# Moving the first 8 MB load ahead of the program's opening barrier in a ReLU-and-row-sum kernel

## The chip, the cores and the metric

The kernel runs on one core of one Trainium2 chip. The metric is the device time of one execution in microseconds (us).

"Span" is the time from the first to the last of the program's own instructions in the profile. A semaphore is a counter that an engine raises, or waits for: in the trace of the kernel before SyncE's drain at 0.00 us raises one, and its barrier instruction at 0.65 us waits for another. A packet is one piece of a DMA transfer as the profiler recorded it.

## The reference

```python
x = randn(32, 512, 1024)            # float32, 67.11 MB
out = sum(maximum(x, 0), axis=-1)   # (32, 512) float32
```

The 16,384 rows are laid out as 128 partitions of 128 rows each. One row has 1,024 numbers, 4 KB.

## The kernel before

The kernel streams the input through two buffers of 16 rows per partition (8 MB each). SyncE issues every load. ScalarE takes the even rows and VectorE the odd ones; each instruction applies the ReLU and sums a row. The last rows come in smaller loads, so that little work is left after the last one lands.

```python
    big = 16
    tail = [8, 4, 2, 1]
    pieces = [244, 252, 260, 268]
    ...
    io_pool = ctx.enter_context(tc.tile_pool(name="io", bufs=2))
    ...
    for j, cpd in enumerate(chunks):
        ...
        nc.sync.dma_start(
            out=xt,
            in_=xv[:, m0 * D : (m0 + cpd) * D].rearrange("p (c d) -> p c d", c=cpd),
        )
        for c in range(cpd):
            ...
            elif (c % 2) == 0:
                act_op(xt[:, c, :], xt[:, c, :], m)
            else:
                dve_op(xt[:, c, :], xt[:, c, :], res[:, m : m + 1])
```

The program has an opening that the kernel's author doesn't write. GpSimd sets four small constants. Then all five engines meet in a barrier: the other four each run an instruction called drain, which adds one to a semaphore, and wait; GpSimd sees that the four have come (at 0.53 us in the trace of the kernel before) and releases them (at 0.61). Only then do the engines branch to the kernel's body, whose first SyncE instruction is the first load.

## Time and profile before

| | before |
|---|---|
| device time, median of the first 3 runs | 164.37 us |
| span in the profile | 162.7 us |
| SyncE's first load issued | 0.73 us after the span's start |
| first DMA packet starts | 1.74 us |
| all of the first load landed | 23.18 us |

The page of the kernel before, cut to four lines: the span; each engine's busy time with its share of the span and its instructions; SyncE's DMA queue with packets, MB and the share of 16 engines' span; and what was moved:

```profile
span 162.7 us, 347 instructions
...
DVE 74.3 (46%) x134; ACT 69.0 (42%) x129; POOL 0.2 (0%) x4
...
q1 hardware_dynamic: 2304, 67.11, 96.4%
...
HBM read 67.11 MB, written 0.07 MB: 413 GB/s over the span
```

The compute engines (DVE is VectorE, ACT is ScalarE) are idle more than half of the time. SyncE's DMA queue is busy for 96.4% of all that 16 DMA engines could do. This kernel is a stream, and the stream is what must end earlier.

The timeline of the kernel before, first 3 us. Columns: start, duration, engine, line, operation, operands, count, and in brackets the engine's idle time with what ended it:

```profile
0.24 0.10 POOL L113 MEMSET const-float32-0.0<- 128x1 f32 x1 [0.24 <-issue]
...
0.72 1.28 ACT L41 ACT_TABLE_LOAD   x1 [0.72 <-PEq L113]
0.73 0.85 SPq L65 DMA_DIRECT2D xt<-in_x_dram  x2
```

Nothing moves before 0.73 us: the constants are set from 0.24 us on, and ScalarE and SyncE both start just after the barrier. "SPq" is SyncE's sequencer; the line merges the issues of the first two loads.

The view of waits of SyncE's queue, kernel before. Columns: total, how often, longest:

```profile
SPq L65 <- DVE xt L49: 126.5, 6, 30.8
...
SPq L113 <- PEq L113: 0.7, 1, 0.7
```

The 126.5 us are waits for a free buffer. They look large and cost nothing: the third load is issued at 32.5 us, ten us before the second one has landed (42.7 us), so the DMA engines never run dry (their busy share from 40 to 150 us is 0.99). The 0.7 us wait in the barrier is small, and it is the one that matters, because nothing at all is queued while it lasts.

### The profile page before, as it was taken

The page shows a single profiled execution, that of the slowest core. Times are in us where ns is not written, and L with a number is a line of the kernel's source. Part 1 is how long each engine was busy: PE and PEld are TensorE (multiplying, and loading weights), DVE is VectorE, ACT ScalarE, POOL GpSimd, SP SyncE. Part 2 cuts the span into 40 slices and gives each one's busy share as a digit, 9 for nine tenths or more (in the row PEclk, how much of TensorE's full clock was granted, in tenths as well). Part 3 has the DMA queues.
Part 4 walks back from the last instruction along what each step waited for, and adds up shares of the span by engine and source line. Part 5 has one row for each costly group of instructions (what it writes and reads, how often), then busy time and mean ns, then how long its engine had stood idle before and what let it go on. Part 6 is the DMA issues. An engine that isn't in the chain of part 4 may idle for free.

```text
span 162.7 us, 347 instructions
## 1 busy us (share of the span) xinstructions
DVE 74.3 (46%) x134; ACT 69.0 (42%) x129; POOL 0.2 (0%) x4
## 2 busy tenths in 40 slices
DVE  0000029900597007950099300992039900598983
ACT  3000029700595007930099100990039700596882
POOL 0000000000000000000000000000000000000000
DMA  7969969969969979979989998998997997999990
GB/s 258 483 290 516 499 274 516 499 274 516 500 274 516 516 306 467 516 338 435 516 356 421 499 403 387 516 419 354 516 467 306 516 467 306 451 443 395 405 362 23
DMA packets 2450, 67.19 MB, mean 413 GB/s; under 512 B 528, under 2 KB 1040, under 8 KB 1168
## 3 DMA queue, kind: packets, MB, share of 16 engines
q1 hardware_dynamic: 2304, 67.11, 96.4%
q10 hardware_dynamic: 144, 0.06, 0.1%
q14 instruction: 2, 0.02, 0.0%
HBM read 67.11 MB, written 0.07 MB: 413 GB/s over the span
## 4 chain that ended last, share of the span: by engine, by line
DMA 78%; DVE 18%; SPq 1%; issue 0%; DVEq 0%
DMA xt<-in_x_dram 62%; DVE xt L49 17%; DMA p<-in_x_dram 17%; SPq L65 1%; DVE p L49 1%; DVEq L49 0%; DVEq L124 0%
## 5 line engine op out<-in xcount | busy, mean ns | idle before, releaser
L49 DVE TENSOR_SCALAR_CACHE_REDUCE xt<-xt 128x1024 f32<-128x1024 f32 x63 | 72.6, 1215 | 85.7 <-DMA xt<-in_x_dram 85.4
L41 ACT ACTIVATE xt<-xt 128x1024 f32<-128x1024 f32 x64 | 66.7, 1043 | 90.3 <-DMA xt<-in_x_dram 90.3
L41 ACT ACTIVATION_READ_ACCUMULATOR xt<-xt 128x1 f32 x64 | 11.9, 186 | 0.0
L49 DVE DVE_READ_ACCUMULATOR xt<-xt 128x1 f32 x63 | 5.2, 83 | 0.0
L49 DVE TENSOR_SCALAR_CACHE_REDUCE p<-p 128x244 f32<-128x244 f32 (+3 forms) x4 | 1.6, 420 | 0.5 <-DMA p<-in_x_dram 0.4
L41 ACT ACT_TABLE_LOAD x1 | 1.3, 1283 | 0.7 <-PEq L113 0.7
L49 DVE DVE_READ_ACCUMULATOR p<-p 128x1 f32 x4 | 0.3, 83 | 0.0
L113 POOL MEMSET const-bfloat16-1.0<- 128x1 bf16 x1 | 0.1, 102 | 0.0
L113 POOL MEMSET const-uint8-127<- 128x1 uint8 x1 | 0.1, 101 | 0.0
L113 POOL MEMSET const-float32-0.0<- 128x1 f32 x1 | 0.1, 99 | 0.2 <-issue 0.2
L113 POOL MEMSET const-float32-1.0<- 128x1 f32 x1 | 0.1, 98 | 0.0
## 6 DMA issues: line engine op xcount, KB each, us to landing
xt<-in_x_dram SPq DMA_DIRECT2D x1, 4096.0 KB, 19.7
xt<-in_x_dram SPq DMA_DIRECT2D x1, 2048.0 KB, 24.2
xt<-in_x_dram SPq DMA_DIRECT2D x1, 1024.0 KB, 26.2
xt<-in_x_dram SPq DMA_DIRECT2D x1, 512.0 KB, 27.0
p<-in_x_dram SPq DMA_DIRECT2D x1, 134.0 KB, 10.0
p<-in_x_dram SPq DMA_DIRECT2D x1, 130.0 KB, 26.5
p<-in_x_dram SPq DMA_DIRECT2D x1, 126.0 KB, 26.7
p<-in_x_dram SPq DMA_DIRECT2D x1, 122.0 KB, 26.9
```

The lines of the kernel that those rows point to most:

```text
L41: nc.scalar.activation(out=out_ap, in_=in_ap, func=mybir.ActivationFunctionType.Relu, accum_out=res[:, m : m + 1],)
L49: nc.vector.tensor_scalar(out=out_ap, in0=in_ap, scalar1=0.0, scalar2=None, op0=mybir.AluOpType.max, op1=mybir.AluOpType.add, accum_out=ac ...
L65: nc.sync.dma_start(out=xt, in_=xv[:, m0 * D : (m0 + cpd) * D].rearrange("p (c d) -> p c d", c=cpd),)
L113: nc = _bacc.Bacc("TRN2", target_bir_lowering=False, num_devices=1)
```

## The change

The intent is to hide the opening barrier. By the program, the first load needs nothing that the barrier protects: its buffer is untouched, its source is an input, and its semaphore is at zero. (That is reasoning.) So its issue is taken out of the body once the program has been compiled, and put ahead of SyncE's drain in the opening.

```diff
+EARLY = 1
+
+def tile_relu_sum_kernel(tc, x, out):
+    trace_relu_sum(tc, x, out)          # the old kernel function, renamed
+    tc.close()
+    tc.compile()
+    issue_ahead_of_the_barrier(tc, EARLY)
+
+def issue_ahead_of_the_barrier(tc, n_loads):
+    SP = mybir.EngineType.SP
+    blocks = tc.nc.main_func.blocks
+    opening = blocks[0].instructions
+    body = next(b for b in blocks if b.name == tc.start_bb_name).instructions
+    loads = [i for i in body if i.engine == SP][:n_loads]
+    for i in loads:
+        assert isinstance(i, mybir.InstDMACopy)
+        body.remove(i)
+    at = next(n for n, i in enumerate(opening)
+              if i.engine == SP and isinstance(i, mybir.InstDrain))
+    opening[at:at] = loads
```

(Blank lines, type annotations and line breaks are left out here. In this diff and those below, what stands behind a # was added for this document.) No instruction is added or taken away: both profiles count 347.

More of the change, by code (lines that the diff above doesn't have):

```diff
@@ L6, with kernel, issue_ahead_of_the_barrier, trace_relu_sum @@
 from concourse._compat import with_exitstack
+EARLY = 1
+def kernel(tc: tile.TileContext, x: bass.AP, out: bass.AP):
+    trace_relu_sum(tc, x, out)
+    tc.close()
+    tc.compile()
+    issue_ahead_of_the_barrier(tc, EARLY)
+def issue_ahead_of_the_barrier(tc: tile.TileContext, n_loads: int):
+    SP = mybir.EngineType.SP
[6 more added lines that the diff above has]
+        body.remove(i)
+    at = next(
+        n
+        for n, i in enumerate(opening)
+        if i.engine == SP and isinstance(i, mybir.InstDrain)
+    )
+    opening[at:at] = loads
 @with_exitstack
-def kernel(
+def trace_relu_sum(
     ctx: ExitStack,
```

## The prediction

Two passages are cut from it, as marked. 164.37 us, less 0.73 us for the moved issue, plus up to 0.05 us for a colder first issue, is about 163.7 us.

> **What bounds the kernel now.** It is a stream: the page shows 67.11 MB read, the DMA queue of SyncE busy for 96.4% of 16 engines' span of 162.7 us, VectorE 46% and ScalarE 42%. In the steady part the packet records show 64 KB packets of 2.42 us on each of 16 engines, which is 433 GB/s[...]. At 433 GB/s the 67.11 MB take 155 us, so about 7.7 us of the span are start, ramp and tail. The view of waits shows compute waiting for loads (85.4 us VectorE, 90.3 us ScalarE). SyncE's queue waits 126.5 us for buffers, but the third load is issued 10 us before the second has landed (32.5 against 42.7 us), the later ones likewise, so the engines always have a load queued.
>
> **The start.** In the trace SyncE is the first engine in the program: its part of the opening barrier is at 0.00 us, VectorE's, ScalarE's and GpSimd's first instructions at 0.13, PE's at 0.32. GpSimd then sets four constants (0.24 to 0.43), drains until 0.48, gathers at 0.53 and releases at 0.61; SyncE passes at 0.65. It issues the first load at 0.73 (0.38 us, timeline) and the first packet starts at 1.74, 1.01 us after the issue began.[...]
>
> **The change** adds and removes no instruction; it moves the first load's issue from 0.73 us to SyncE's first slot, about 0.00. Removed from the critical path: 0.73 us. Cost: SyncE now arrives at the barrier after its 0.38 us issue, near 0.40 instead of 0.00. PE arrives at 0.32 and GpSimd looks only at 0.53, so the release should stay at 0.61. The second load stays at about 0.73 us, long before it is needed.
>
> The load's start heads a stream without gaps, so all of it should shift rigidly: first landing (before: 23.2 us) to about 22.45, the third load's issue from 32.5 to about 31.75, and the end likewise. Ramp and tail stay. Gain 0.73 us, less perhaps 0.05 for a colder first issue (estimate: the first issue takes 0.38 us, the third 0.33).
>
> **Prediction: 163.7 us** (164.37 less about 0.7, 0.4%), range 163.3 to 164.3. Chances: faster by over 2% 0.01, within 2% 0.98, slower by over 2% 0.01.
>
> **What would show it.** Right: first load issued within 0.1 us of the span's start, first packet near 1.0 us, barrier release still near 0.6 us, the landings and the last instruction 0.6 to 0.75 us earlier, span near 162.0, steady rate unchanged. Wrong: release of the barrier later by the issue's 0.38 us (costs nothing unless it is much more); first packet further than 1.1 us behind its issue; the shift present at the first landing and gone by the last one.
>
> **What would make it wrong.** (a) SyncE's drain in the barrier waits until the 8 MB have landed: then all engines start near 22 us, the second load is issued only then, and the DMA engines idle for one issue-to-packet latency, about 1 us net. (b) In the timed executions another engine enters first, or the metric's clock starts so as to hide the gain. (c) An engine-level straggler or a fetch of instructions near the end absorbs it. (d) Drift between runs: 0.3% is 0.5 us, nearly the effect.

## The result, and the profile after

Ratios below are the mean time of one kernel's fast runs over that of the other's of the same rounds, so they are not quite the ratio of the medians that stand beside them.

| | before | after |
|---|---|---|
| device time, median (lowest to highest), 4 runs each | 164.34 (164.23 to 164.52) | 163.32 (163.30 to 163.39) |
| ratio | | 0.9941 (0.9927 to 0.9955) |
| span in the profile | 162.7 | 161.5 |
| first load issued | 0.73 | 0.00 |
| first DMA packet starts | 1.74 | 1.02 |
| first load landed | 23.18 | 22.24 |

The page of the changed kernel:

```profile
span 161.5 us, 347 instructions
...
DVE 74.3 (46%) x134; ACT 69.0 (43%) x129; POOL 0.2 (0%) x4
...
q1 hardware_dynamic: 2304, 67.11, 96.9%
...
HBM read 67.11 MB, written 0.07 MB: 416 GB/s over the span
```

The same work and the same bytes in a span that is 0.7% shorter. The interval of the ratio excludes 1, and this gain is what is explained here. The timeline of the changed kernel, first 3 us:

```profile
0.00 1.11 SPq L95 DMA_DIRECT2D xt<-in_x_dram  x2
0.23 0.10 POOL L143 MEMSET const-float32-0.0<- 128x1 f32 x1 [0.23 <-issue]
...
0.78 1.28 ACT L71 ACT_TABLE_LOAD   x1 [0.78 <-PEq L143]
```

The first issue is now the first thing that happens. The barrier opens slightly later: ScalarE's table load begins at 0.78 us where it began at 0.72. In the trace's records SyncE's drain behind the issue takes 0.13 us, so SyncE reaches the barrier at 0.56 us and has become the last to arrive. And SyncE's queue hardly waits in the barrier any more (view of waits, SyncE's queue, changed kernel):

```profile
SPq L95 <- DVE xt L79: 125.8, 6, 30.4
...
SPq L143 <- PEq L143: 0.2, 1, 0.2
```

So the mechanism looks as forecast. The size doesn't quite: 1.02 us were gained in the medians and 1.17 us between the two profiles, and the issue moved by only 0.73 us. The timelines of both kernels at the first landing, before and then after, show that more than 0.73 us has gone by then:

```profile
23.20 1.22 DVE L49 TENSOR_SCALAR_CACHE_REDUCE xt<-xt 128x1024 f32<-128x1024 f32 x1 [23.20 <-DMA xt<-in_x_dram]
```

```profile
22.27 1.22 DVE L79 TENSOR_SCALAR_CACHE_REDUCE xt<-xt 128x1024 f32<-128x1024 f32 x1 [22.27 <-DMA xt<-in_x_dram]
```

That is 0.93 us. The rest is in the stream itself. Here is the view by windows, 40 to 150 us, of before, then of after (columns: window, its length, busy time and count of VectorE, ScalarE, GpSimd, granted clock, DMA share, GB/s):

```profile
40.00:150.00 110.00, 55.37 (x97) 50.72 (x97) 0.00 (x0) 1.00 0.99 427
```

```profile
40.00:150.00 110.00, 56.55 (x99) 51.90 (x99) 0.00 (x0) 1.00 1.00 432
```

The stream of this one profile of the kernel before ran at 427 GB/s and that of the changed kernel at 432. Nothing in the change touches this stretch. Either these extra 0.3 to 0.4 us are scatter, or the opening has an effect on the stream that I had not seen. That is the question for the experiments.

### The profile page after: what moved, and what is told of

Same layout as the page of the kernel before. It is cut to its first block, busy times and chain, and to the rows that moved or that the text cites. A ratio compares the mean times of both kernels' runs of the same rounds, so it can differ in the third digit from the quotient of the medians.

```text
span 161.5 us, 347 instructions
## 1 busy us (share of the span) xinstructions
DVE 74.3 (46%) x134; ACT 69.0 (43%) x129; POOL 0.2 (0%) x4
## 4 chain that ended last, share of the span: by engine, by line
DMA 79%; DVE 18%; SPq 1%; issue 0%; DVEq 0%
DMA xt<-in_x_dram 62%; DVE xt L79 17%; DMA p<-in_x_dram 17%; SPq L95 1%; DVE p L79 1%; DVEq L79 0%; DVEq L16 0%
## 5 line engine op out<-in xcount | busy, mean ns | idle before, releaser
L79 DVE TENSOR_SCALAR_CACHE_REDUCE xt<-xt 128x1024 f32<-128x1024 f32 x63 | 72.6, 1216 | 84.5 <-DMA xt<-in_x_dram 84.2
```

Of the source, the lines that this page charges most:

```text
L79: nc.vector.tensor_scalar(out=out_ap, in0=in_ap, scalar1=0.0, scalar2=None, op0=mybir.AluOpType.max, op1=mybir.AluOpType.add, accum_out=ac ...
```

## The experiments

**Theory A.** The whole stream shifts rigidly with the first issue; only the time of that issue counts. What is beyond 0.73 us is scatter, of the profile of before and of its runs.

**Theory B.** The order of the opening also changes how fast the first loads run. In the kernel before the second issue follows the first at once (0.43 us from start to start); in the changed one it stands 0.78 us behind it. A second issue close behind might slow the first load.

**Theory C.** Being ahead of the barrier helps by itself, whatever the time of the issue, through what runs beside the first packets.

An overview; times in us. "Issue" and "barrier" (when ScalarE passes it) are from each run's trace, "landed" is the landing of the first 8 MB less the time of the first issue.

| run | issue | barrier | landed | median (lowest to highest) | ratio to before |
|---|---|---|---|---|---|
| e1: before, unchanged | 0.73 | 0.65 | 22.31 | 163.90 (163.76 to 164.17) | 0.9986 |
| e4: before, gap between the issues | 0.73 | 0.65 | 22.43 | 164.18 (163.89 to 164.32) | 0.9995 |
| e6: early, held back | 0.58 | 1.28 | 22.52 | 163.98 (163.78 to 164.26) | 0.9993 |
| e5: load late | 3.01 | 0.65 | 22.53 | 166.38 (166.35 to 166.84) | 1.0145 |
| e2: after, unchanged | 0.00 | 0.69 | 22.40 | 163.32 (163.26 to 163.80) | 0.9954 |
| e10: after, unchanged | 0.00 | 0.71 | 22.27 | 163.20 (163.15 to 163.28) | 0.9948 |
| e3: two early | 0.00 | 1.17 | 22.24 | 163.38 (163.14 to 163.49) | 0.9950 |
| e7: barrier late | 0.00 | 2.98 | 22.23 | 163.50 (163.40 to 163.63) | 0.9963 |
| e9: small first load | 0.00 | 1.17 | 21.62 | 163.36 (162.98 to 163.67) | 0.9958 |
| e8: two queues | 0.00 | 1.41 | 42.76 | 183.49 (183.20 to 183.63) | 1.1178 |

All gave correct results. The kernel before, run beside them, had medians of 164.19 (e1 to e4), 164.13 (e5 to e8) and 164.13 (e9, e10).

### e1 and e2: both kernels again

No edit. Expected of e1:

> The kernel before, unchanged, run as if it were a change, to see how much its runs, spans and first landing scatter. The move of the issue explains 0.73 us; 1.02 us was measured, and the two profiles differ by 1.17 us in span: 0.73 in the issue, 0.21 more by the first landing, 0.15 more by the second. Theory A (only the shift of the issue counts; the rest is scatter of the one profile and of the runs of before): this run's profile differs from the first one by 0.2 us or more in span, and issue to first landing is anywhere between 22.2 and 22.5 us. Theory B (the opening's order also changes how fast the first loads run): issue to first landing is again 22.4 to 22.5 us, span again 162.6 to 162.8, ratio 1.000.

Expected of e2:

> The changed kernel again, on the same chip as the others. Both theories: about 163.3 us, span 161.5. Theory B: issue to first landing again 22.2 to 22.3 us; theory A: it may be anything from 22.2 to 22.5.

Measured: e1 has a span of 162.1 us in its profile, 0.6 us less than the first profile of the very same program. The ratio of e1 to the same kernel beside it is 0.9986 (0.9972 to 1.0000), so even the means of a batch differ by 0.2 us. First issue to first landing is 22.31 us, not the 22.45 of the first profile; it lies between the changed kernel's 22.24 and 22.40. The same window of e1:

```profile
40.00:150.00 110.00, 55.98 (x97) 51.34 (x97) 0.00 (x0) 1.00 0.99 429
```

and of e2, the changed kernel again:

```profile
40.00:150.00 110.00, 56.05 (x97) 51.39 (x97) 0.00 (x0) 1.00 1.00 430
```

The streaming rate is 427 and 429 GB/s in two profiles of before, 432 and 430 in two of after: the ranges nearly meet, and in e2 the profiled run was the slowest span of its five (162.0; the others 161.5 to 161.7). The first profile of before, 162.7, was slower than all 34 later runs of that kernel (162.0 to 162.6). Of e2's expectation, the 163.3 us came true; its profiled run had a span of 162.0 where 161.5 was expected, and 22.40 us to the first landing where theory B asked for 22.2 to 22.3. This speaks for theory A: most of the extra gain of the first comparison was one unlucky profile and a high batch. Why that batch of the kernel before lay high is not known.

### e3: two loads ahead of the barrier

```diff
-EARLY = 1
+EARLY = 2
```

> Both of the first two loads are issued ahead of the barrier, back to back as in the kernel before (about 0.43 us apart; 0.78 in the changed kernel). Theory A (pure shift): 163.3 us, as the changed kernel, since the second load is not needed for 20 us. Theory B (a second issue close behind the first slows the start of the first load): issue to first landing back to 22.4 to 22.5 us, about 163.6 us.

Measured: 163.38 us, and 22.24 us to the first landing, with the two issues 0.42 us apart. Timeline of e3:

```profile
0.00 0.84 SPq L95 DMA_DIRECT2D xt<-in_x_dram  x2
...
1.24 1.28 ACT L71 ACT_TABLE_LOAD   x1 [1.24 <-PEq L143]
```

The issues are as close together as before the change, and the gain is still there. Theory B's prediction (163.6 us) is missed. The barrier now opens about half a us later than in the changed kernel and that isn't seen in the time either.

### e4: a gap between the issues, behind the barrier

The first load is put behind SyncE's part of the barrier, and a pause of seven empty drains follows it:

```diff
+    for _ in range(7):                 # made before the tile context
+        nc.sync.drain()
...
-    at = next(
+    at = 1 + next(
...
-        if i.engine == SP and isinstance(i, mybir.InstDrain)
+        if i.engine == SP and isinstance(i, mybir.InstEventSemaphore)
```

> The first load stays behind the barrier, and seven empty drain instructions on SyncE stand between it and the second one, so that the two issues are about 0.8 us apart as in the changed kernel. Theory A: 164.3 us, as before. Theory B: about 164.05 us, issue to first landing 22.2 to 22.3 us.

Measured: 164.18 us (before beside it: 164.19), 22.43 us to the first landing, issues 0.91 us apart. Timeline of e4, the two issues and VectorE's first work:

```profile
0.73 1.24 SPq L95 DMA_DIRECT2D xt<-in_x_dram  x2
...
23.18 1.22 DVE L79 TENSOR_SCALAR_CACHE_REDUCE xt<-xt 128x1024 f32<-128x1024 f32 x1 [23.18 <-DMA xt<-in_x_dram]
```

A gap alone brings nothing. Theory B falls with e3 and e4 together: the spacing was taken from either kernel into the other, and the time stayed with the time of the first issue.

### e5: the load much later

```diff
+    for _ in range(44):                # behind the barrier, ahead of the first load
+        nc.sync.drain()
     with _tile.TileContext(nc) as tc:
```

> The kernel before with 44 empty drain instructions on SyncE between the barrier and the first load's issue; seven of them took 0.48 us in the last batch, so the issue should be about 3.0 us later, at 3.75 us. Theory A (the stream shifts rigidly with the first issue): 3.0 us slower than before, 167.2 us, spans and landings all 3.0 us later. Rival (some of the issue's time is hidden, or is paid more than once): a slope clearly off 1, under 2.6 or over 3.4 us.

Measured: 166.38 against 164.13 us, 2.25 us slower. The expectation of 3.0 us was wrong, and 2.25 us even lies below the 2.6 us that it set as the mark of a rival; but both were worked out for a move of 3.0 us, and the issue moved less. A drain took 0.052 us here, not the 0.069 that I had worked out from e4 (where the first one stands behind an issue; in the changed kernel such a drain takes 0.13 us). The timeline of e5 shows where the issue and the first landing came to be:

```profile
3.01 0.84 SPq L65 DMA_DIRECT2D xt<-in_x_dram  x2
...
25.56 1.22 DVE L49 TENSOR_SCALAR_CACHE_REDUCE xt<-xt 128x1024 f32<-128x1024 f32 x1 [25.56 <-DMA xt<-in_x_dram]
```

The issue moved by 2.28 us (3.01 less 0.73), the time by 2.25 us in the medians and 2.4 us by the ratio (1.45% of 164.13). The slope that theory A asks for is 1, and it is 1 within the scatter.

### e6: ahead of the barrier, but not earlier

Eleven drains ahead of the early load:

```diff
-    opening[at:at] = loads
+    opening[at:at] = pauses + loads    # pauses: 11 drains, moved here from behind the barrier
```

> The changed kernel, but eleven empty drains stand ahead of the early load, so it stays ahead of SyncE's part of the barrier and is issued at about 0.75 us, as in the kernel before; the barrier then opens at about 1.3 us. Theory A (only the time of the issue counts): 164.2 us, as before, issue-to-first-landing 22.2 to 22.5. Rival C (being ahead of the barrier helps by itself, by what runs beside the first packets, such as the table load of ScalarE): about 163.9 us or less.

Measured: 163.98 us against 164.13 for before beside it, ratio 0.9993 (0.9980 to 1.0006). The drains held it less than meant: the issue stands at 0.58 us, so 0.15 us of the move were left, and theory A with that time gives 163.98. Timeline of e6:

```profile
0.58 1.10 SPq L99 DMA_DIRECT2D xt<-in_x_dram  x2
1.35 1.28 ACT L75 ACT_TABLE_LOAD   x1 [1.35 <-PEq L147]
```

The load is ahead of the barrier in program order, the table load comes well behind the issue, and the gain is gone but for what the 0.15 us explain. Theory C expected about 163.9 us or less for a full hold of 0.75 us. As the hold was shorter, A and C come within 0.1 us of each other here, and this run doesn't separate them as sharply as meant; it leaves C no effect larger than the scatter.

### e7: the barrier much later, the load not

```diff
-    opening[at:at] = loads
+    opening[at:at] = loads + pauses    # pauses: 44 drains
```

> The changed kernel with 44 empty drains between the early load and SyncE's part of the barrier: the load is issued at 0.00 as in the changed kernel, and all engines and the second load are held until about 3.6 us instead of 0.7. Theory A: 163.3 us, as the changed kernel, since no engine is needed before the first landing at 22.2 us and no second load before about 20 us. Rival (the barrier's time is on the path): up to 3 us slower.

Timeline of e7:

```profile
0.00 3.38 SPq L99 DMA_DIRECT2D xt<-in_x_dram  x2
...
3.05 1.28 ACT L75 ACT_TABLE_LOAD   x1 [3.05 <-PEq L147]
...
22.26 1.22 DVE L83 TENSOR_SCALAR_CACHE_REDUCE xt<-xt 128x1024 f32<-128x1024 f32 x1 [22.26 <-DMA xt<-in_x_dram]
```

Measured: 163.50 us. The barrier opened 2.3 us later than in the changed kernel and the second load was issued at 3.06 us; VectorE's first work begins at 22.26 us, as in the changed kernel (22.27). The 0.18 us above the changed kernel's 163.32 are no more than two batches of one kernel differ by (e1). With e5 this is the clearest pair: 2.3 us of delay in front of the load cost 2.25 us, 2.3 us of delay behind it cost 0.18 us, which the scatter can account for.

### e8: two queues (a try for a faster version, failed)

In the traces the 16 DMA engines take their first packets over 0.9 to 1.3 us. I tried to shorten this ramp with a second issuer.

```diff
+        if j == 0:
+            nc.sync.dma_start(out=xt[0:64], in_=src[0:64])
+            nc.scalar.dma_start(out=xt[64:128], in_=src[64:128])   # both ahead of the barrier
```

From the expectation a condition is cut that named a cause of the ramp.

> A try for a faster version: the first load is split by partitions, 0 to 63 issued by SyncE and 64 to 127 by ScalarE, both ahead of the barrier. In the traces so far the 16 DMA engines take their first packet over 0.9 to 1.3 us after the first of them. [...]two queues shorten it and the first landing comes up to 0.4 us earlier: about 163.0 us. If it doesn't, 163.3 us.

Measured: 183.49 us, 19 us slower. The page of e8, GB/s in 40 slices of the span, and the two queues:

```profile
GB/s 231 231 231 231 231 231 216 188 173 346 462 462 462 433 418 375 390 462 462 462 462 433 418 364 404 462 462 462 447 447 404 404 375 462 418 433 393 417 391 40
...
q1 hardware_dynamic: 2240, 62.92, 86.3%
q10 hardware_dynamic: 224, 4.26, 11.0%
```

The first load moved at half rate until about 40 us, 231 GB/s in most slices where later ones have up to 462: its 64 KB packets took 4.92 us where others take 2.42. The packet records of e8 show that its two halves were moved in turns: 16 packets of SyncE's queue start at 1.34 to 2.00 us, then 16 of ScalarE's at 5.89 to 7.21 us, then 16 of SyncE's at 10.82 to 12.14 us, and so on in eight such turns. Why a packet takes twice as long in them was not shown: e8 has both a cut by partitions and a second queue, and no run has one without the other. The expectation had thought of neither the turns nor the longer packets: it was about how soon the first packets start.

### e9 and e10: a small first load, and the changed kernel once more

The same ramp, cut by rows instead of partitions, on the one queue:

```diff
-EARLY = 1
+EARLY = 2
...
+        if j == 0:
+            nc.sync.dma_start(out=xt[:, 0:2, :], in_=src[:, 0:2, :])
+            nc.sync.dma_start(out=xt[:, 2:cpd, :], in_=src[:, 2:cpd, :])
```

> A second try for a faster version: the first load is cut by rows, 2 rows of each partition (8 KB pieces, 1 MB) and then 14 rows, both issued by SyncE ahead of the barrier on the one queue. In the changed kernel the first 64 KB packets take 3.0 us in the mean, the later ones 2.42, and the 16 engines start theirs over 0.9 to 1.3 us. If the ramp grows with the size of the first pieces, all engines are running full earlier and the first landing of all 16 rows comes up to 0.4 us before 22.2 us: about 163.0 us. If it is a fixed latency of the first pieces, 163.3 us.

> The changed kernel a third time, on the same chip as the cut load. From the eight kernels so far (two queues left out) the time is 163.4 us plus 1.02 us for each us by which the first issue is later; this one should be 163.3 to 163.5 us, ratio to before 0.994 to 0.997.

Measured: e9 163.36 us (162.98 to 163.67), e10 163.20 us. The first 8 MB did land earlier, at 21.62 us where e10 has 22.27, and yet the time is no better. Timelines of e9 and of the first profile of the changed kernel, at the start of work on the first full load and on the fifth:

```profile
21.64 1.22 DVE L79 TENSOR_SCALAR_CACHE_REDUCE xt<-xt 128x1024 f32<-128x1024 f32 x1 [15.72 <-DMA xt<-in_x_dram]
...
100.24 1.22 DVE L79 TENSOR_SCALAR_CACHE_REDUCE xt<-xt 128x1024 f32<-128x1024 f32 x1 [10.76 <-DMA xt<-in_x_dram]
```

```profile
100.27 1.22 DVE L79 TENSOR_SCALAR_CACHE_REDUCE xt<-xt 128x1024 f32<-128x1024 f32 x1 [10.63 <-DMA xt<-in_x_dram]
```

The lead was 0.63 us at the first load (21.64 against 22.27) and 0.03 us at the fifth. By the semaphores, the 16 engines of e9 finish the first load within 0.37 us of each other and the fifth within 1.04 us; in the changed kernel it is 0.96 and 1.43. So the landing of a load is set by the engine that is last, and the cut evened the engines out for a while. The lead over the changed kernel at the landings of the first five 8 MB was 0.62, 0.54, 0.28, 0.15 and 0.03 us. What spreads the engines again was not tested, but for the last step the traces show a candidate. The page of e9 (and, with the same count of two, of the kernels before and after) lists a queue of the kind "instruction", to which no line of the kernel issues anything:

```profile
q14 instruction: 2, 0.02, 0.0%
```

In all eleven traces with one queue at the start, its two packets of 8 KB run between 84.2 and 90.2 us, and at the end of each one (within 0.01 us) a 64 KB packet starts that takes 2.67 to 3.02 us instead of 2.42. There the fifth 8 MB land 19.48 to 19.96 us after the fourth; the sixth land only 19.34 to 19.36 us after the fifth. Both kernels have this (19.88 us before, 19.84 after), so it does not enter the comparison, but at up to 0.6 us it is as large as the gains sought here. e10 came out at 163.20 us, 0.1 us below the stated range, and inside it by the ratio (0.9948).

### All runs together

A straight line through the 72 timed runs of the first comparison's "after", e1 to e7, e10 and the kernel before beside them (0.73 us taken as its issue time; the batches stood on three chips, and the kernel before had means within 0.13 us on all three) gives 163.36 us plus 1.03 us (standard error 0.03) for each us of the first issue's time; the runs scatter by 0.17 us around it. Without the runs of e5, which lie far out, the slope is 1.00 (0.06). For the 0.73 us of the change that is 0.75 us. The means say the same: 164.09 us over 34 runs of the kernel before (e1 and the runs beside the experiments), 163.32 us over 14 runs of the changed one, 0.77 us apart. With a scatter of 0.17 us the standard error of that difference is about 0.05 us (0.17 times the root of 1/34 + 1/14), so it agrees with 0.73.

One thing of theory B's kind remains. From first issue to first landing, the five traces with a whole first load issued at 0.00 (after, e2, e3, e7, e10) have 22.23 to 22.40 us, in the mean 22.28. The five with a later issue (before, e1, e4, e5, e6) have 22.31 to 22.53, in the mean 22.45. That is 0.17 us, and the two groups hardly overlap. It follows neither the spacing of the issues (e3 and e4) nor the place in the program (e6 is ahead of the barrier and has 22.52). I have no tested cause for it. But it doesn't last: counted from the first issue, the two groups differ by 0.17 us at the first landing, 0.10 at the third, 0.05 at the fourth and -0.02 at the fifth, and the last instruction ends 161.69 us behind the first issue in the group at 0.00 and 161.66 in the other. Over the whole program the traces thus show a rigid shift, as theory A says.

## Why the prediction was right

The prediction was 163.7 us in a range of 163.3 to 164.3, "within 2%" at 0.98; measured were 163.32 us and a ratio of 0.9941. It was right, and its mechanism too, but the point lies 0.38 us above the measurement, and 163.32 is only 0.02 us inside the range's lower end. That the range held so narrowly is in part luck: the base lay 0.28 us too high, as shown below. Step by step:

- **The stream bounds the kernel, and it has no gap.** Right. In e5 a delay of the first issue comes out at the end one for one, over 160 us of streaming and eight buffer turns.
- **The move is worth 0.73 us, less perhaps 0.05.** Right: the issue moved from 0.73 to 0.00 us, the first packet from 1.74 to 1.02 (in all eleven traces with one queue at the start it starts 0.98 to 1.02 us after the start of the issue, and 0.62 to 0.65 us after its end), and the pooled runs give 0.75 to 0.77 us. The reserve of 0.05 us for a colder first issue was not needed (0.377 us against 0.376).
- **The base of 164.37 us.** This is the term that was mis-sized. It is the median of three runs which lay high; 34 later runs of the same kernel have a mean of 164.09. These 0.28 us are most of the 0.38; the rest is 0.07 us of gain (0.77 instead of 0.70) and 0.03 of rounding. The prediction named drift of this size as its item (d), but took it for noise on the answer and not for an error of the starting point.
- **The barrier's release stays at 0.61 us, since SyncE arrives at about 0.40.** Wrong by 0.05 us and without effect. SyncE arrives at 0.56, since its drain behind the issue takes 0.13 us, and the release comes at 0.66. e7 shows that even 2.3 us there cost no more than 0.18 us, about the scatter.
- **First landing near 22.45, end 0.6 to 0.75 us earlier, span near 162.0.** The two profiles had 22.24, 1.17 and 161.5, outside of these statements. Over the ten traces with a whole first load on one queue the landing comes 22.23 to 22.53 us behind the issue, where I had taken it as fixed. About 0.17 us of that may go with the issue's time, as told above; that cause stays open, and none of it is left at the fifth landing. The span of before in later runs was 162.0 to 162.6, so most of the 1.17 was the one profile.
- **What would make it wrong.** (a) did not happen: the drain behind an 8 MB issue did not wait for the 8 MB; it took 0.13 us, and they landed 22 us later. (b) did not happen: the metric shows the move in full. (c), that a DMA engine which lags, or a fetch of instructions, absorbs it, did not happen to this change: what looks like such a fetch, at 84 to 90 us, is in the traces of both kernels. But it is like what became of e9.

## What to carry to other kernels

In this kernel, whose DMA queue never runs dry, the first issue is the head of the whole time: 2.28 us put in front of it cost 2.25 us, and the same delay behind it cost no more than the scatter. So, in a kernel of this kind, move loads that depend on nothing ahead of the opening barrier, and expect no more than the time by which the issue moves. To judge a gain of half a percent, run the old kernel again too: its first three runs and its one profile made this one look a third larger than it was.
